# RWKV's beta, k and v turned token-major by 32x32 blocks on VectorE and DMAs, in place of TensorE transposes

## Chip, cores and metric

One NeuronCore of a Trainium2 chip. The metric is the device time of one execution in microseconds; runs are summed up by their median. The engines are PE (TensorE, matrix products), ACT (ScalarE), DVE (VectorE), POOL (GpSimd) and SP (SyncE, which issues nearly all DMAs here).

## What is computed

One layer of a streaming encoder over 512 tokens of width 2048, in float32. An input projection feeds two branches, RWKV-7 time mixing (16 heads of 64) and HGRN2 (8 heads of 128). Their gated outputs go through an output projection, and a layer norm of the residual ends it. Cut to the part that the change touches:

```python
proj = einsum('btd,dc->btc', h, w_in)          # 512 x 2048 by 2048 x 8320
r, k, v, z, wd, ad = split(token_shift(proj[..., :RWKV_COLS]))
kk = normalize(k * k_k);  k = k * (1 + (a - 1) * k_a)
# per head, token by token, state S of 64 x 64:
#   S = S * w_t + (S @ -kk_t) (kk_t * a_t)^T + v_t k_t^T ;  o_t = S @ r_t
y = einsum('btc,cd->btd', concatenate([o_rwkv, o_hgrn], -1), w_out)
out = layer_norm(ALPHA * x + y)
```

The recurrence is evaluated by chunks of 64 tokens. Within a chunk the kernel needs the vectors beta (kk scaled by a and by the decay), k and v with tokens on the partitions, while the projection leaves them with channels on the partitions.

## The kernel before

**Main products.** Projections and the output projection are made in a split form: each operand is a rounded high part and a low rest, and three 128x512 matmuls (line 431, in `three`) make one product. 3900 such matmuls run. Weights come from DRAM in 156 loads of 512 KB (`load`, L408) into two buffers `wr`. Each load is split by halves: ACT makes `wh` (L330), DVE makes `wl` (L340), with three buffers of each. A half feeds 12 main matmuls. A load is issued when the second half of the one two before it is split.

**Side work.** RWKV's heads are treated as 8 pairs, two pairs to a group. `rwkv_prep` makes a pair's operands: `ar` holds kappa and r, `bk` holds beta and k, each [128 channels, 8 chunks, 128]; 16 score products of `bk` and `ar` follow. Then `bk` and v are brought to tokens on partitions (L699 to L729), the latter into rows 64 to 127 of `z`. `rwkv_group` inverts the chunks' triangular matrices by some 60 short DVE operations with block transposes (L359), then `rwkv_scan` walks the 8 chunks, reading `z` and `bk`, and `outputs` and `rwkv_finish` make the gated output `g`. HGRN heads run beside this. For the output projection each gated output is split again into `gh` (tiles named `xh`) and `gl` (`xl`).

**Order.** All instructions are put out by a planner (`Plan`, L63). Python generators yield operations with costs. The planner keeps a clock per engine. Between any two main matmuls it puts out those side operations that would be ready, queue by queue. Engines then run their own lists in order and wait on semaphores. Tiles are taken from counted buffers by `room` and `take`: `q4` has 6 (`ar` and `bk` of two pairs hold 4 until the scan of their group ends, HGRN takes 2), `ksq` 2, `zz` 2, PSUM `mix` and `main` 4 each. The transposes of `bk` and v were PE operations `tr` (L321, against the identity in `cst`) into `mix`, followed by copies (`copy`, L377: ACT or DVE, whichever the planner finds earlier).

**The end.** Pair 7 is prepared last. Its gated output is the last of the 16 that the output projection takes; the first quarter of that projection takes one of them every 12 main matmuls.

Of the kernel before, what the change touches and what calls it, by code (L numbers as in the profile page):

```python
# [15 lines left out]
P = 128  # L16
# [7 lines left out]
NCH = T // C  # L24
# [210 lines left out]
def mixer_kernel(ctx, tc, head, x_r, w_all, par, up, ln_wb, consts, hmask, out):  # L235
    nc = tc.nc
    pe, sc_e, dve, pool = nc.tensor, nc.scalar, nc.vector, nc.gpsimd
# [9 lines left out]
    def nm(s):  # L247
        uid[0] += 1
        return f"{s}{uid[0]}"
# [5 lines left out]
    plan = Plan({**BUFS, **PBUFS})  # L255
    tags = {}

    def st(tag, shape, dt=F32):
        return spool.tile(shape, dt, tag=tag, name=nm(tag), bufs=BUFS[tag])

    def take(tag, shape=(P, T), dt=F32):

        if not plan.free(tag):
            raise RuntimeError(f"no room: {tag}")
        slot = min(plan.slots[tag])
        plan.slots[tag].remove(slot)
        if tag in PBUFS:
            t = ppool.tile(list(shape), dt, tag=tag, name=nm(tag), bufs=PBUFS[tag])
            plan.banks.add(t.tensor.name)
        else:  # L270
            t = st(tag, list(shape), dt)
        name = t.tensor.name
        plan.busy[name] = (slot[1], None)
        tags[name] = tag
        return t

    def drop(*tiles):
        for t in tiles:
            name = t.tensor.name
            plan.slots[tags.pop(name)].append((plan.used.get(name, plan.count), plan.busy[name][0]))  # L280

    def room(**need):

        return lambda: all(plan.free(tag, n) for tag, n in need.items())

    def has(S, *names):
        return lambda: all(n in S for n in names)

    def landed(*tiles):

        names = [getattr(t, "tensor", t).name for t in tiles]

        def test():
            now = plan.clock["pe"] + plan.LEAD
            if not plan.free("mix") or min(plan.slots["mix"])[1] + 0.15 > now:
                return False
            return all(n in plan.ready and plan.seen(n, "pe") <= now for n in names)

        return test


    def size(ap):
        n = 1
        for s in ap.shape[1:]:
            n *= s
        return n
# [13 lines left out]
    def tr(o, i):  # L320
        return Op([("pe", 0.11, lambda: pe.transpose(o, i, ident))], [i], [o])  # L321

    def moved(o, i):

        return 0.1 if o.shape[0] < P else 0.0

    def act_way(o, i, f, scale=1.0, bias=0.0):
        cost = 0.09 + size(o) * 0.00085 + moved(o, i) + (0.06 if isinstance(scale, bass.AP) else 0.0)
        if f == AF.Copy:
            return "act", cost, lambda: sc_e.activation(o, i, f, scale=scale)  # L330
        return "act", cost, lambda: sc_e.activation(o, i, f, scale=scale, bias=bias)  # L331
# [4 lines left out]
    def dve_op(reads, o, f, n=None, per=0.00104, base=0.07):  # L336
        return Op([("dve", base + (n or size(o)) * per, f)], reads, [o])
# [20 lines left out]
    def dtr(o, i):  # L358
        return dve_op([i], o, lambda: dve.transpose(o, i), per=0.0019)  # L359
# [17 lines left out]
    def copy(o, i, scale=1.0):  # L377

        if scale != 1.0:
            f = lambda: dve.tensor_scalar(o, i, scale, None, ALU.mult)  # L380
        else:
            f = lambda: dve.tensor_copy(o, i)
        return Op([act_way(o, i, AF.Copy, scale), ("dve", 0.075 + size(o) * 0.00105 + moved(o, i), f)], [i], [o])

    splits = plan.queue()
# [48 lines left out]
    def by_now(t):  # L436

        n = t.tensor.name
        return n in plan.ready and plan.seen(n, "pe") <= plan.clock["pe"] + plan.LEAD
# [8 lines left out]
    def main_ps(tags=("main",)):  # L448

        def test():  # L450
            now = plan.clock["pe"]
            return [t for t in tags if plan.free(t) and min(plan.slots[t])[1] + 0.15 <= now]

        plan.until(test)
        return take(min(test(), key=lambda t: min(plan.slots[t])[1]))

    def proj(u, hook=None):

        ps = main_ps()
        for j in range(4):  # L460
            if hook:
                hook(j)
            hi, lo = part(4 * u + j, P)
            for kk in range(4):
                if kk == 1:
                    ready(4 * u + j + 1)
                if kk == 2:
                    ready(4 * u + j + 2)
                k = 4 * j + kk
                three(ps, hi[:, kk], lo[:, kk], xh[k], xl[k], k == 0, k == KT - 1)  # L470
        return ps
# [24 lines left out]
    def unit(n=1):  # L496
        u = nunit[0]
        nunit[0] += n
        return u
# [54 lines left out]
    def chunks(t):  # L554
        return t.rearrange("p (c s) -> p c s", s=C)
# [46 lines left out]
    def rwkv_prep(S, p):  # L602
# [5 lines left out]
        bk = take("q4", [P, NCH, 2 * C])  # L608
        a, sg, kx2 = take("t"), take("t"), take("t")
# [6 lines left out]
        for i, (o, xs, low, h) in enumerate(((sg, wah, wlo, HW0), (a, aah, alo, HA0))):  # L616
# [3 lines left out]
            ps = take("mix")  # L620
# [48 lines left out]
        o = S["ot"] = take("t")  # L669
# [17 lines left out]
        pss = [take(tag) for tag in ("main", "mix") for h in range(2)]  # L687
# [8 lines left out]
            drop(ps)  # L696
        S["scored"] = True

        yield room(mix=2)  # L699
        pss = [take("mix") for _ in range(2)]  # L700
        for c in range(NCH):
            yield tr(pss[c // 4][:, c % 4 * P : (c % 4 + 1) * P], bk[:, c])
        for i, ps in enumerate(pss):
            yield copy(bk[:, 4 * i : 4 * i + 4], tiles(ps))
            drop(ps)
        yield has(S, "v")
        yield room(ksq=2)
        rh, rl = (take("ksq", [P, T], F32R) for _ in range(2))
# [6 lines left out]
        v = S["v"]  # L715
# [3 lines left out]

        yield room(zz=1)  # L720
        z = take("zz", [P, NCH, P])
        yield landed(v)
        ps = take("mix")
        for j in range(4):
            yield tr(ps[:, j * P : j * P + P], v[:, j * P : j * P + P])
        for e in range(2):
            yield copy(z[64:128, e::2], tiles(ps)[64 * e : 64 * e + 64])
        drop(ps, v)
        S["zz"] = z  # L729

    def from_v(SS, sc):
# [197 lines left out]
    def tiles(t):  # L929
        return t.rearrange("p (c t) -> p c t", t=P)  # L930
# [239 lines left out]
    pss = [main_ps() for _ in us]  # L1170
# [91 lines left out]
    for name, j in _order()[1:]:  # L1262
# [24 lines left out]
        if name == "k":  # L1287
            plan.add(preps, rwkv_prep(SS[j], j))
            if j % 2 == 1:
                plan.add(groups, rwkv_group(SS[j - 1 : j + 1], j // 2))  # L1290
# [3 lines left out]
        if (name, j) in (("k", 0), ("r", 0)):  # L1294
            ps = pss["wkr".index(name)]
        else:
            ps = proj(unit(), begin_out if (name, j) == ("z", NPAIR - 1) else None)
# [199 lines left out]
    pss = []  # L1497
# [51 lines left out]
    for t in range(4):  # L1549
        sl = slice(t * P, t * P + P)  # L1550
        ps = main_ps(banks if t == 3 else banks)
# [12 lines left out]
        for i in range(2):  # L1564
            c = slice(i * T // 2, i * T // 2 + T // 2)
# [85 lines left out]
```

## Time and profile before

| what | value |
|---|---|
| median of 3 runs | 1061.66 us (1061.06 to 1062.9) |
| profiled execution, its time | 1061.85 us |
| its span | 1060.1 us |
| PE busy | 1052.2 us (99%) |
| DVE busy | 749.0 us (71%) |
| ACT busy | 454.4 us (43%) |
| DMA packets | 35078, of which 4144 under 512 B |

The page gives one profiled execution. Busy times are unions of an engine's instructions; a PE matmul's duration includes its latency, so that matmuls overlap and PE's occupancy is read from the distance of their starts. A row of a group reads: line, engine, operation, tile written <- tiles read, shapes, count, busy us, mean ns, idle time before and what ended it. A row of the timeline begins with the start and the duration in us. A tile is named by its buffer tag, so `t`, `q` (of `q4`) or `ksq` stand for many tensors.

### The profile page before, as it was taken

What the parts mean: (1) busy time and instruction counts of PE and PEld (TensorE: products, weight loads), DVE (VectorE), ACT (ScalarE), POOL (GpSimd) and SP (SyncE); (2) the same over time, 40 slices, a digit from 0 to 9 for tenths busy, and PEclk for the clock granted to TensorE, in tenths of its full rate; (3) what the DMA queues carried; (4) which work ended last, traced back from release to release, by engine and by line L of the source; (5) the groups of instructions that cost most, each with busy time, mean ns of one, the idle gap of its engine ahead of it and who ended that gap; (6) DMA issues with size and microseconds to landing.
All of it is one profiled execution on the core that took longest, in us unless ns stands there. A gap on an engine that the chain in (4) does not pass through costs nothing.

```text
span 1060.1 us, 18788 instructions
## 1 busy us (share of the span) xinstructions
PE 1052.2 (99%) x7438; PEld 875.6 (83%) x7438; DVE 749.0 (71%) x1636; ACT 454.4 (43%) x900; POOL 37.4 (4%) x81
## 2 busy tenths in 40 slices
PE   9999999999999999999999999999999999999997
PEld 8888888888888888888888888888888888888885
DVE  7467995567679977676898556766997878525556
ACT  6455434345353355534533434636335454323321
POOL 0000000000100000001000000000000001000000
PEclk9999999999999999999999999999999999999999
DMA  8222222232233312233232222223332245544613
GB/s 329 56 94 85 84 97 81 71 95 80 76 99 90 100 62 86 70 91 95 90 93 87 82 81 85 80 77 94 89 100 61 81 130 176 172 128 150 208 60 129
DMA packets 35078, 108.46 MB, mean 102 GB/s; under 512 B 4144, under 2 KB 5936, under 8 KB 34864
## 3 DMA queue, kind: packets, MB, share of 16 engines
q1 hardware_dynamic: 34848, 107.08, 32.0%
q8 instruction: 58, 0.95, 0.4%
q14 instruction: 28, 0.23, 0.1%
q10 hardware_dynamic: 144, 0.20, 0.1%
HBM read 99.92 MB, written 7.34 MB: 101 GB/s over the span
## 4 chain that ended last, share of the span: by engine, by line
PE 95%; DMA 2%; DVE 2%; ACT 0%; issue 0%; DVEq 0%
PE main L431 70%; PE mix L317 11%; PE mix L431 8%; PE main L1176 3%; DMA wr<-w_all 2%; PE mix L321 2%; PE main L317 2%; DVE wl L340 0%; PE mix L1126 0%; DVE inv L349 0%; DVE t L340 0%; ACT t L330 0%; DVE inv L340 0%; DVE q L349 0%; DVE ia L340 0%
## 5 line engine op out<-in xcount | busy, mean ns | idle before, releaser
L431 PE MATMUL main<-xh,wl 128*128 128x512 f32 x864 | 342.7, 397 | 0.0
L431 PE MATMUL main<-xh,wh 128*128 128x512 f32 x864 | 342.7, 397 | 0.0
L431 PE MATMUL main<-xl,wh 128*128 128x512 f32 x864 | 340.4, 394 | 0.0
L330 ACT ACTIVATE wh<-wr 128x512 fp32r<-128x512 f32 x299 | 186.9, 627 | 175.1 <-PE main L431 123.9
L340 DVE TENSOR_TENSOR wl<-wr,wh 128x512 fp32r<-128x512 f32 x299 | 204.2, 684 | 76.4 <-ACT wh L330 74.8
L431 PEld LDWEIGHTS main<-xh,wl 128*128 128x128 f32 x864 | 162.5, 188 | 33.0 <-DVE wl L340 0.2
L431 PEld LDWEIGHTS main<-xl,wh 128*128 128x128 f32 x864 | 162.5, 188 | 32.1
L431 PEld LDWEIGHTS main<-xh,wh 128*128 128x128 f32 x864 | 162.6, 188 | 31.0
L431 PE MATMUL main<-wh,xh 128*128 128x512 f32 (+1 forms) x262 | 102.2, 390 | 0.0
L431 PE MATMUL main<-wh,xl 128*128 128x512 f32 (+1 forms) x262 | 102.1, 390 | 0.0
L431 PE MATMUL main<-wl,xh 128*128 128x512 f32 (+1 forms) x262 | 101.8, 389 | 0.1
L431 PEld LDWEIGHTS main<-wl,xh 128*128 128x128 f32 x262 | 49.2, 188 | 10.4 <-DVE wl L340 0.5
L431 PEld LDWEIGHTS main<-wh,xl 128*128 128x128 f32 x262 | 49.2, 188 | 10.0
L431 PEld LDWEIGHTS main<-wh,xh 128*128 128x128 f32 x262 | 49.2, 188 | 9.7
L330 ACT ACTIVATE zz<-mix 64x64 f32<-64x64 f32 (+1 forms) x92 | 25.3, 275 | 57.8 <-PE mix L317 38.8
L331 ACT ACTIVATE t<-main,om 128x512 f32<-128x512 f32 x33 | 22.5, 689 | 44.7 <-PE main L431 35.1
L340 DVE TENSOR_TENSOR inv<-inv 64x30 f32<-64x30 f32 (+14 forms) x120 | 38.7, 322 | 3.2
L340 DVE TENSOR_TENSOR inv<-inv,inv 64x30 f32<-64x30 f32 (+14 forms) x120 | 38.7, 322 | 3.1
L349 DVE SCALAR_TENSOR_TENSOR bd<-mix,pc,bd 64x64 f32<-64x64 f32 x112 | 31.7, 283 | 10.0 <-PE mix L317 8.0
L340 DVE TENSOR_TENSOR t<-t,tot 128x256 f32<-128x256 f32 x96 | 37.1, 419 | 0.3
L349 DVE SCALAR_TENSOR_TENSOR t<-main,pr,t 128x511 f32<-128x511 f32 x33 | 24.4, 746 | 16.9 <-ACT t L331 16.7
L331 ACT ACTIVATE t<-main 128x512 f32<-128x512 f32 x32 | 18.7, 597 | 37.9 <-PE main L431 37.8
(223 smaller groups left out, 1344.8 us busy)
## 6 DMA issues: line engine op xcount, KB each, us to landing
wr<-w_all SPq DMA_DIRECT2D x156, 512.0 KB, 3.6
q<-head SPq DMA_DIRECT2D x15, 448.0 KB, 5.6
g<-x_r SPq DMA_DIRECT2D x16, 256.0 KB, 4.0
spill<-g SPq DMA_DIRECT2D x12, 256.0 KB, 4.5
t<-spill SPq DMA_DIRECT2D x12, 256.0 KB, 4.1
out<-q SPq DMA_DIRECT2D x12, 256.0 KB, 2.5
big<-ln_wb SPq DMA_DIRECT2D x1, 2048.0 KB, 8.7
up<-up SPq DMA_DIRECT2D x8, 128.0 KB, 3.6
```

The source lines that it names most:

```text
L317: return Op([("pe", cost, lambda: pe.matmul(o, l, r, start=start, stop=stop, **kw))], [l, r], [o], mode="narrow" if narrow else "main" if ...
L321: return Op([("pe", 0.11, lambda: pe.transpose(o, i, ident))], [i], [o])
L330: return "act", cost, lambda: sc_e.activation(o, i, f, scale=scale)
L331: return "act", cost, lambda: sc_e.activation(o, i, f, scale=scale, bias=bias)
L340: return dve_op([a, b], o, lambda: dve.tensor_tensor(o, a, b, f), base=0.16 if o.shape[0] < P and size(o) == C and o.tensor.name in tags e ...
L349: return dve_op([a, b], o, lambda: dve.scalar_tensor_tensor(o, a, s, b, f1, f2), per=0.00113, base=0.085 if o.shape[0] == P else 0.25 if s ...
L431: pe.matmul(ps, l, r, start=first and i == 0, stop=last and i == 2)
L1176: pe.matmul(pss[a], *ops, start=k == 0 and low == of == 0, stop=k == KT - 1 and low == 1)
```

## The change

`rwkv_prep` no longer transposes on PE. A new helper, `turned`, transposes every 32x32 block of a tile in one DVE instruction into a scratch tile, and then moves the blocks to their places by DMAs from SP, SBUF to SBUF: 16 DMAs for `bk` (in place, scratch from `q4`) and 8 for v (into rows 64 to 127 of `z`, scratch from `ksq`). Each DMA moves 32 partitions by 8 chunks by 32 floats, 32 KB in rows of 128 B. The planner is told to put out one column of blocks (4 or 2 DMAs), then to let 0.4 us per DMA pass, and takes the result for ready 3.0 us after the last.

```diff
+    def turned(dst, src, tmp, rows=4, base=0):
+        name = dst.tensor.name
+        yield dtr(tmp, src)
+        yield lambda: by_now(tmp)
+        for a in range(4):
+            for b in range(rows):
+                o = base + 32 * b
+                nc.sync.dma_start(dst[o : o + 32, :, 32 * a : 32 * a + 32],
+                                  tmp[32 * a : 32 * a + 32, :, 32 * b : 32 * b + 32])
+            at = plan.clock["pe"] + 0.4 * rows
+            yield lambda: plan.clock["pe"] >= at
+        plan.ready[name] = (plan.clock["pe"] + 3.0, "dma")
...
-        yield room(mix=2)
-        pss = [take("mix") for _ in range(2)]
-        for c in range(NCH):
-            yield tr(pss[c // 4][:, c % 4 * P : (c % 4 + 1) * P], bk[:, c])
-        for i, ps in enumerate(pss):
-            yield copy(bk[:, 4 * i : 4 * i + 4], tiles(ps))
-            drop(ps)
+        yield room(q4=1)
+        tmp = take("q4", [P, NCH, P])
+        yield from turned(bk, bk, tmp)
+        drop(tmp)
...
-        yield landed(v)
-        ps = take("mix")
-        for j in range(4):
-            yield tr(ps[:, j * P : j * P + P], v[:, j * P : j * P + P])
-        for e in range(2):
-            yield copy(z[64:128, e::2], tiles(ps)[64 * e : 64 * e + 64])
-        drop(ps, v)
+        yield room(ksq=1)
+        tmp = take("ksq")
+        yield from turned(z, chunks(v), chunks(tmp), rows=2, base=64)
+        drop(v, tmp)
```

Since the planner decides the order, three places are shown; line numbers after the change are higher by 15 up to the helper's callers.

PE, behind the last score product of pair 0 (`mix_704`), before:

```order
L317 MATMUL mix_704<-q_446,q_447 128x128
L431 MATMUL main_649<-xh_79,wl_661 128x512
L431 MATMUL main_649<-xh_80,wh_680 128x512
L431 MATMUL main_649<-xl_96,wh_680 128x512
L431 MATMUL main_649<-xh_80,wl_681 128x512
L321 MATMUL mix_735<-cst,q_447 128x128 x4
L321 MATMUL mix_736<-cst,q_447 128x128 x4
L431 MATMUL main_649<-xh_81,wh_680 128x512
```

and after:

```order
L317 MATMUL mix_704<-q_446,q_447 128x128
L446 MATMUL main_649<-xh_79,wl_661 128x512
L446 MATMUL main_649<-xh_80,wh_680 128x512
L446 MATMUL main_649<-xl_96,wh_680 128x512
L446 MATMUL main_649<-xh_80,wl_681 128x512
L446 MATMUL main_649<-xh_81,wh_680 128x512
```

The eight transposes of `bk` (`q_447`) are gone and the main matmuls follow one another.

SP's queue around the same pair, with the semaphores that each issue waits for (`DMAHW0` to `DMAHW7` are the eight that DMAs use in turn), before:

```order
L408 DMA wr_685<-w_all 128x1024 [waits DMAHW4_49,DVE_49]
L408 DMA wr_767<-w_all 128x1024 [waits DMAHW5_49,DVE_49]
L408 DMA wr_821<-w_all 128x1024 [waits DMAHW6_49,DVE_49]
L596 DMA up_826<-up 128x256 [waits DMAHW2_49]
L408 DMA wr_876<-w_all 128x1024 [waits DMAHW7_49,DVE_49]
```

and after (the first block DMA waits for PE's scores, which read the tile that it overwrites):

```order
L423 DMA wr_751<-w_all 128x1024 [waits DMAHW5_49,DVE_49]
L394 DMA q_447<-q_735 32x8x32 [waits PE_49]
L394 DMA q_447<-q_735 32x8x32
L394 DMA q_447<-q_735 32x8x32 [waits DMAHW2_49,PE_49]
L394 DMA q_447<-q_735 32x8x32 x3
L394 DMA q_447<-q_735 32x8x32 [waits DMAHW6_49]
L394 DMA q_447<-q_735 32x8x32 [waits DMAHW7_49]
L423 DMA wr_794<-w_all 128x1024 [waits DMAHW0_49,DVE_49]
L394 DMA q_447<-q_735 32x8x32 [waits DMAHW1_49]
L394 DMA q_447<-q_735 32x8x32 [waits DMAHW2_49]
L394 DMA q_447<-q_735 32x8x32 [waits DMAHW3_49]
L394 DMA q_447<-q_735 32x8x32 [waits DMAHW4_49]
```

Eight block DMAs now stand between two weight loads, and each waits for the DMA eight before it.

DVE at the end of the side work, where pair 7's gated output (`g_9174` before) is made and the output projection's splits `wl` and `xl` alternate, before:

```order
L340 TENSOR_TENSOR t_7497<-t_7497,sm_9088 128x512
L340 TENSOR_TENSOR xl_9184<-t_9066,xh_9183 128x512
L349 SCALAR_TENSOR_TENSOR g_9174<-mix_9190,half,t_7405 128x512
L349 SCALAR_TENSOR_TENSOR t_8993<-ksq_9175,t_8993 128x512
L340 TENSOR_TENSOR wl_9202<-wr_9111,wh_9201 128x512
L349 SCALAR_TENSOR_TENSOR g_9174<-g_9174,half,t_8993 128x512
L340 TENSOR_TENSOR xl_9213<-t_9092,xh_9212 128x512
L340 TENSOR_TENSOR wl_9223<-wr_9111,wh_9222 128x512
L340 TENSOR_TENSOR xl_9235<-t_9121,xh_9234 128x512
L340 TENSOR_TENSOR wl_9247<-wr_9171,wh_9246 128x512
```

and after (`g_9369` is the same output):

```order
L340 TENSOR_TENSOR t_7607<-t_7607,sm_9275 128x512
L340 TENSOR_TENSOR wl_9374<-wr_9269,wh_9373 128x512
L349 SCALAR_TENSOR_TENSOR g_9369<-mix_9385,half,t_7437 128x512
L340 TENSOR_TENSOR xl_9393<-g_9241,xh_9392 128x512
L349 SCALAR_TENSOR_TENSOR t_8925<-ksq_9370,t_8925 128x512
L340 TENSOR_TENSOR wl_9406<-wr_9318,wh_9405 128x512
L349 SCALAR_TENSOR_TENSOR g_9369<-g_9369,half,t_8925 128x512
L340 TENSOR_TENSOR xl_9417<-g_9154,xh_9416 128x512
L340 TENSOR_TENSOR wl_9429<-wr_9318,wh_9428 128x512
L340 TENSOR_TENSOR xl_9441<-g_9369,xh_9440 128x512
```

Before, the split `xl` of that output comes further down, behind seven pairs of `xl` and `wl` from the last operation on `g_9174`; after, it is the third row behind it. The finish of the last pair has moved later against the output projection by about six of its steps.

## Prediction

> **What bounds the kernel now.** I read the page first, then the groups of instructions with shapes kept apart, then the transposes' own line, then the timeline around one use of each kind, then SyncE's (SP's) issues.
>
> ```profile
> span 1060.1 us, 18788 instructions
> PE 1052.2 (99%) x7438; PEld 875.6 (83%) x7438; DVE 749.0 (71%) x1636; ACT 454.4 (43%) x900; POOL 37.4 (4%) x81
> DVE  7467995567679977676898556766997878525556
> PE 95%; DMA 2%; DVE 2%; ACT 0%; issue 0%; DVEq 0%
> L431 PEld LDWEIGHTS main<-xh,wl 128*128 128x128 f32 x864 | 162.5, 188 | 33.0 <-DVE wl L340 0.2
> ```
>
> PE is busy for 99% of the span and makes 95% of the chain that ended last. The last row is the check on it: the loads of the low weight halves, which DVE makes, had to wait for DVE 0.2 us in the whole run. The planner keeps PE fed, so what leaves PE leaves the time, unless something else starts to make PE wait. DVE is at 9 tenths in some slices, so there it has little to give.
>
> The profiled execution took 1061.85 us: the span of 1060.1 and 1.75 around it. It lies 0.2 above the median of the runs shown (1061.66); I sum against it. A measurement of this kernel can tell about 0.2%, 2.1 us, from no change.
>
> **What leaves PE.** All transposes stand on one line. The timeline shows one set of eight (beta and k) and one of four (v) on PE, and two splits of weights on ACT that follow PE at its own pace:
>
> ```profile
> L321 PE MATMUL mix<-cst,t x120: 270/272/329, 77.6 to 891.3; 128*128 128x128 f32 x120
> L321 PE MATMUL mix<-cst,q x64: 270/272/273, 72.3 to 751.6; 128*128 128x128 f32 x64
> L321 PEldq EVENT_SEMAPHORE  x13: 51/51/51, 181.1 to 877.7; - x13
> ...
> 105.37 0.39 PE L431 MATMUL main<-xl,wh 128*128 128x512 f32 x1
> 105.59 1.04 PE L321 MATMUL mix<-cst,q 128*128 128x128 f32 x8
> 106.39 0.48 PE L431 MATMUL main<-xh,wl 128*128 128x512 f32 x1
> 106.70 0.40 PE L431 MATMUL main<-xh,wh 128*128 128x512 f32 x1
> ...
> 113.28 0.40 PE L431 MATMUL main<-xh,wl 128*128 128x512 f32 x1
> 113.51 0.60 PE L321 MATMUL mix<-cst,t 128*128 128x128 f32 x4
> 113.87 0.48 PE L431 MATMUL main<-xh,wh 128*128 128x512 f32 x1
> 114.19 0.39 PE L431 MATMUL main<-xl,wh 128*128 128x512 f32 x1
> 907.28 0.63 ACT L330 ACTIVATE wh<-wr 128x512 fp32r<-128x512 f32 x1 [1.56 <-PE main L431]
> 910.00 0.63 ACT L330 ACTIVATE wh<-wr 128x512 fp32r<-128x512 f32 x1 [1.56 <-PE main L431]
> ```
>
> Of the 184 transposes, all 64 of the `q` row and 32 of the `t` row go (8 pairs by 8 and by 4). Their 272 ns is latency, not occupancy: eight take 1.04 us together. What one set costs is read from the starts of the main matmuls. Undisturbed, a half-load of 12 of them lasts 2.72 us (907.28 to 910.00), so they start 0.23 us apart. From 105.37 to 106.70 lie two main starts and eight transposes: 1.33 - 2 x 0.23 = 0.87 us, the slower restart after the switch included. From 113.28 to 114.19: 0.91 - 0.46 = 0.45 us. Eight pairs: 8 x (0.87 + 0.45) = **10.56 us off PE**. The Trainium skill (TensorE: Matmul & The Clock Gate, Part 4: PE-mode transpose) gives about 275 ns for a transpose inside a kernel; taken as PE time, 96 of them would be 26 us and the sum about 1038. The trace agrees with that figure as a duration (272 ns) and not as a price, so the sum goes by the starts.
>
> The copies from PSUM go too. They were off the path.
>
> ```profile
> L330 ACT ACTIVATE q<-mix 128x512 f32<-128x512 f32 x13 | 7.2, 596 | 49.5 <-PE mix L321 49.5
> L330 ACT ACTIVATE zz<-mix 64x512 f32<-64x512 f32 x14 | 8.3, 592 | 18.3 <-PE mix L321 14.2 <-DVE zz L382 4.1
> L359 DVE STREAM_TRANSPOSE inv<-big 32x1024 f32<-32x1024 f32 x8 | 16.3, 2039 | 0.2
> L340 DVE TENSOR_TENSOR wl<-wr,wh 128x512 fp32r<-128x512 f32 x299 | 204.2, 684 | 76.4 <-ACT wh L330 74.8
> ```
>
> ACT loses 15.5 us, worth nothing at 43% busy.
>
> **What DVE gets.** Per pair one block transpose of 1024 columns and one of 512. The nearest row has 1024 columns on 32 partitions, 2.04 us; twice the 512-column row below it would be 1.37. I take 2.04 for 128 partitions, the same operation, and half, 1.02, for v. That is 8 x 3.06 = 24.5 us, less the five copies that ACT did not do, at 0.68 like the other 512-column rows: 3.4. DVE rises by 21 to 770 us, 73%. Its cover is the splitting ahead: three buffers of 2.72 us each are in turn, so a 2.04 us block fits before the next `wl` is due. The HGRN heads take the scratch buffer next, and their first copies, on DVE or ACT in front of the next splits, wait for the last block DMAs: landed 3.6 us after issue at the weights' price (below), freed by the planner after 1.6, so 2 us in each of four groups at most. Where DVE is at 9 tenths it may not. Bounds: nothing, or all that the four odd pairs add (each sits where its group's inversion runs), 4 x 3.06 = 12.2 us. I take 1.0 with this wait in it, near the low end, by the 0.2 us row.
>
> **What SP gets.** 24 DMAs per pair of 32 KB, each waiting for the one eight before it, with weight loads queued behind. The planner spaces them 0.4 us apart.
>
> ```profile
> 13.80 0.53 SPq L529 DMA_DIRECT2D cst<-consts  x1
> 14.38 0.45 SPq L529 DMA_DIRECT2D ksq<-hmask  x1
> ...
> cst<-consts SPq DMA_DIRECT2D x1, 208.0 KB, 5.0
> ksq<-hmask SPq DMA_DIRECT2D x1, 40.0 KB, 4.6
> wr<-w_all SPq DMA_DIRECT2D x156, 512.0 KB, 3.6
> ...
> L408 SPq DMA_DIRECT2D wr<-w_all x156: 327/328/423, 16.9 to 1000.0; - x156
> L1135 SPq DMA_DIRECT2D q<-head x15: 327/328/739, 1.6 to 18.1; - x15
> 351.01 0.33 SPq L408 DMA_DIRECT2D wr<-w_all  x1
> 356.25 0.63 ACT L330 ACTIVATE wh<-wr 128x512 fp32r<-128x512 f32 x1 [2.08 <-PE main L431]
> ```
>
> An issue takes SP 0.33 us, 0.42 when pressed, 0.74 at most. Packets: the mask's 128 rows of 320 B landed at 14.38 + 4.6 = 18.98, the constants queued ahead of them at 18.80; 0.18 us for 8 rows on each of 16 engines, 22 ns a row. A new DMA has 256 rows of 128 B, 16 per engine, at most 0.35 us by that price. So both fit the 0.4 us spacing. How late may a weight load be? The one issued at 351.01 landed at about 354.6, was first read at 356.25 because ACT waited for PE to free a buffer, and its product is due two half-loads later (5.44 us), less the split (0.63 + 0.68): 1.6 + 4.1 = 5.7 us of cover. At 0.42 us an issue, 16 DMAs put SP 0.3 us behind; at 0.74, 5.4 us. I take nothing, with 0 and 20 us as ends (8 pairs by 24 x 0.74 - 9.6 - 5.7 = 2.5).
>
> **What PE gets.** The first products from each `z` now wait for up to eight DMA semaphores. One such wait costs PE's queue 51 ns (row above): 64 of them 3.3 us, or nothing where a 0.23 us matmul runs over them. I take 1.0.
>
> The blocks' own landing is hidden: between the prep of a pair and its scan lies the group's inversion on DVE. In the first group the second pair's v was turned at 113.5, and the scan's first product came at 197.6:
>
> ```profile
> L317 PE MATMUL mix<-rt,big x128: 270/275/347, 197.6 to 867.4; 128*128 128x128 f32 x128
> ```
>
> **The tail.** Pair 7 ends last, and its gated output is the last to be split for the output projection:
>
> ```profile
> 890.96 0.60 PE L321 MATMUL mix<-cst,t 128*128 128x128 f32 x4
> 910.54 0.62 ACT L330 ACTIVATE xh<-g 128x512 fp32r<-128x512 f32 x1
> L349 DVE SCALAR_TENSOR_TENSOR g<-mix,half,t 128x512 f32<-128x512 f32 x16 | 11.9, 747 | 6.7 <-PE mix L321 6.5
> ```
>
> Its last transposes end at 891.56, three DVE operations of 0.75 later (893.8) it is whole, and it is split at 910.54: 16.7 us to spare. In the order of before, seven pairs of `wl` and `xl` stand between; now one (the order shown with the change). Six steps of 2.72 us, 16.3, are gone, since pacing, landing and a fuller DVE push the prep of every pair back. About 0.4 us is left. If the plan is right PE does not wait; I take 0.5, with 0 and 6 (two steps) as ends.
>
> **Sum:** 1061.85 - 10.56 + 1.0 (DVE) + 0 (SP) + 1.0 (semaphores) + 0.5 (tail) = **1053.8 us**. Its own range: 1051.3 with no cost, to 1059 with the tail's 6.
>
> **Rivals.**
> *Weight loads late (slower).* If a block DMA costs SP or the rings c, 16 put SP 16 x (c - 0.4) behind, and beyond 5.7 PE waits, 8 times. The gain is gone at 16 x (c - 0.4) - 5.7 = 1.32, c = 0.84. At c = 1.0 it is 1053.8 + 8 x 3.9 = 1085. For: nothing with 256 rows is in the trace, and small DMAs spread over 32 partitions only. Against: the 0.33 and 22 ns rows. 0.08.
> *Rows of 128 B pay double (slower).* A packet of q1 takes 32.0% x 16 x 1060.1 us / 34848 = 156 ns for 3.07 KB (queue row below), 26 ns for 512 B; if a row of 128 B costs a 512 B read and write, 52 ns, a DMA holds the rings 0.83 us: 16 are 6.9 us behind, 1.2 us of stall a pair, 1063.4 if the queue drains before z, and with z's eight 3.4 us more each, 1091. The Trainium skill (DMA: Bandwidth & Descriptors, Specifications) states 512 B as the least for line rate, with a read-modify-write below. The mask's 320 B rows at 22 ns speak against it here. 0.05.
>
> ```profile
> q1 hardware_dynamic: 34848, 107.08, 32.0%
> ```
>
> *DVE becomes the bound.* All 12.2 us of the odd pairs land on PE: 1061.85 - 10.56 + 12.2 + 1.5 = 1065.0. For: the 9s in DVE's row. Against: 0.2 us of waiting now. 0.10, half of it within 2.1 us since part would still be hidden.
> *The tail decides.* The last group is late by x beyond its 0.4 us and PE waits: 1053.3 + x; x = 8.5 gives 1061.8. For: 16 us of cover spent. Against: the inversion, not a DMA, sets the group's start, and its operations have known times. 0.09, a third each side.
> That the change does nothing is out: the order has 96 transposes fewer.
>
> **Chances.** Forecast 0.68. Faster by over 0.2%: 0.68 + 0.03 = 0.71. Within 0.2%: 0.05 of DVE + 0.03 of the tail = 0.08. Slower: 0.08 + 0.05 + 0.05 + 0.03 = 0.21. The range, 1051 to 1064, holds the forecast, most of the tail and the lower half of the DVE case.
>
> **What would show it.** Right: L321 falls to 88 matmuls, DVE's block transposes rise from 20 to 36, packets to about 87,300 (192 DMAs of 256 rows and 16 semaphores each), PE busy near 1044 and still 99%, and no ACT `wh` group with DMA `wr` among its releasers beyond a few us. Wrong: PE idle before `main` for DVE `wl` (DVE), ACT `wh` waiting for DMA `wr` (SP, rings), an issue of L394 over 0.84 us, or a gap in PE near 890 to 905 ended by `xl<-g` (tail).

## The result and the profile after

Median 1054.11 us (four runs, 1053.71 to 1054.39) against 1061.92 us before (1061.06 to 1062.9): ratio 0.9926, 95% interval 0.9909 to 0.9943, so 7.8 us faster. Measured once more later: 1053.75 against 1061.84, ratio 0.9916 (0.9903 to 0.993). The forecast was 1053.8. The number was right; the experiments show that it was right partly because errors in it cancelled.

The profiled execution of after took 1053.89 us with a span of 1052.1. These are lines of its page, in the order of those shown of before: span, engines, packets, the main queue, and the chain that ended last.

```profile
span 1052.1 us, 18837 instructions
PE 1042.6 (99%) x7342; PEld 867.6 (82%) x7342; DVE 755.1 (72%) x1653; ACT 438.0 (42%) x867; POOL 37.4 (4%) x81
DMA packets 87305, 114.79 MB, mean 109 GB/s; under 512 B 56368, under 2 KB 58160, under 8 KB 87088
q1 hardware_dynamic: 87072, 113.39, 36.5%
PE 99%; DVE 1%; issue 0%; DVEq 0%
```

PE has 96 products fewer and is still busy for 99% of a shorter span: what left PE left the time. DVE rose by 6 us only, where 21 were forecast. The packets are the forecast ones (87,300), and they came cheap: q1's packets took 36.5% x 16 x 1052.1 = 6144 us against 32.0% x 16 x 1060.1 = 5428 before, 717 us more for 52,224 more packets, 14 ns for a row of 128 B. The forecast took 22 as an upper price, and the rival of the double price 52. As an estimate, a quarter of the 26 ns that 512 B of the other packets take would be 6.5, so the short rows cost about twice their share by bytes.

The groups by line and form show the price of each new operation: the block transposes on DVE, and the block DMAs as SP issues them (their line is L394; the weights' DMAs are on L423 now, the main products on L446 and L1185).

```profile
L359 DVE STREAM_TRANSPOSE q<-q 128x1024 f32<-128x1024 f32 x8 | 9.9, 1233 | 0.0
L359 DVE STREAM_TRANSPOSE ksq<-t 128x512 f32<-128x512 f32 x8 | 5.6, 699 | 0.0
```

```profile
L394 SPq DMA_DIRECT2D q<-q x128: 585/608/1749, 75.7 to 769.3; - x128
L394 SPq DMA_DIRECT2D zz<-ksq x64: 585/608/2078, 87.5 to 778.6; - x64
DMA to landing us min/median/max: 1.9/2.5/4.9
```

A block transpose of 1024 columns took 1.23 us, not the 2.04 of the row taken for it. An issue of a block DMA took SP 0.61 us, not 0.33 to 0.42. SP's timeline around the second pair's prep shows what that does to the weights:

```profile
75.67 5.33 SPq L394 DMA_DIRECT2D q<-q  x8
81.10 0.54 SPq L423 DMA_DIRECT2D wr<-w_all  x1
81.69 5.16 SPq L394 DMA_DIRECT2D q<-q  x8
...
87.54 5.96 SPq L394 DMA_DIRECT2D zz<-ksq  x8
```

Eight moves hold SP for 5.2 to 6.0 us where the planner reckoned 3.2, so the weight load behind each eight is late. In the waits, ScalarE's `wh` (the high half of the weights) waits for the weights' DMA six times, 21.5 us together; before it was twice, 3.5 us:

```profile
ACT wh L330 <- DMA wr<-w_all: 21.5, 6, 6.0
PEld mix L317 <- issue: 7.6, 18, 2.1
```

No wait of PE for a weight half follows from it: the lateness ends inside the cover. The second row is the only new stall of PE, 2.1 us in one piece ended by "issue", that is by nothing that the profile shows. It stands in PE's timeline in the middle of a burst of narrow HGRN products (128 products of 16 columns on 32-column weights):

```profile
815.47 0.70 PE L317 MATMUL mix<-t 128*32 128x16 f32 x62
...
816.04 0.45 PE L317 MATMUL mix<-t,t 128*32 128x16 f32 x33
818.54 0.44 PE L317 MATMUL mix<-t,t 128*32 128x16 f32 x29 [2.05 <-issue]
818.90 0.58 PE L446 MATMUL main<-xh,wl 128*128 128x512 f32 x1
...
821.42 0.63 PE L446 MATMUL main<-xh,wh 128*128 128x512 f32 x1
821.85 0.63 PE L446 MATMUL main<-xl,wh 128*128 128x512 f32 x1
...
822.66 0.40 PE L446 MATMUL main<-xh,wh 128*128 128x512 f32 x1
```

After the gap the main products start 0.43 us apart instead of 0.23, half speed, until 822.66. In the trace's packets a transfer of 16 KB on the instruction queue (q8, called a refill below) starts at 816.34, just as PE stops, and ends at 817.27; PE goes on 1.27 us later.

### The profile page after: what moved, and what is told of

It reads as the page before. It is cut to its first block, busy times and chain, and to the rows that moved or that the text cites. A ratio compares the mean times of both kernels' runs of the same rounds, so it can differ in the third digit from the quotient of the medians.

```text
span 1052.1 us, 18837 instructions
## 1 busy us (share of the span) xinstructions
PE 1042.6 (99%) x7342; PEld 867.6 (82%) x7342; DVE 755.1 (72%) x1653; ACT 438.0 (42%) x867; POOL 37.4 (4%) x81
## 3 DMA queue, kind: packets, MB, share of 16 engines
q1 hardware_dynamic: 87072, 113.39, 36.5%
## 4 chain that ended last, share of the span: by engine, by line
PE 99%; DVE 1%; issue 0%; DVEq 0%
PE main L446 74%; PE mix L317 11%; PE mix L446 8%; PE main L1185 3%; PE main L317 2%; PE mix L321 1%; PE mix L1135 0%; DVE inv L349 0%; DVE inv L340 0%; DVE stats L1542 0%; DVEq L1656 0%; DVE mv L1350 0%; DVE mv L345 0%; DVE inv L1133 0%; DVE mv L349 0%
## 5 line engine op out<-in xcount | busy, mean ns | idle before, releaser
L446 PE MATMUL main<-xh,wl 128*128 128x512 f32 x864 | 342.4, 396 | 0.0
L446 PE MATMUL main<-xh,wh 128*128 128x512 f32 x864 | 341.6, 395 | 0.0
L446 PE MATMUL main<-xl,wh 128*128 128x512 f32 x864 | 340.9, 395 | 0.0
L446 PEld LDWEIGHTS main<-xh,wl 128*128 128x128 f32 x864 | 162.7, 188 | 33.0
L446 PEld LDWEIGHTS main<-xl,wh 128*128 128x128 f32 x864 | 162.7, 188 | 32.8
L446 PEld LDWEIGHTS main<-xh,wh 128*128 128x128 f32 x864 | 162.8, 188 | 32.6
L446 PE MATMUL main<-wh,xh 128*128 128x512 f32 (+1 forms) x262 | 102.4, 391 | 0.0
L446 PE MATMUL main<-wh,xl 128*128 128x512 f32 (+1 forms) x262 | 102.1, 390 | 0.0
L446 PE MATMUL main<-wl,xh 128*128 128x512 f32 (+1 forms) x262 | 102.1, 390 | 0.0
L446 PEld LDWEIGHTS main<-wl,xh 128*128 128x128 f32 x262 | 49.2, 188 | 9.8
L446 PEld LDWEIGHTS main<-wh,xl 128*128 128x128 f32 x262 | 49.2, 188 | 9.7
L446 PEld LDWEIGHTS main<-wh,xh 128*128 128x128 f32 x262 | 49.2, 188 | 9.5
L330 ACT ACTIVATE zz<-mix 64x64 f32<-64x64 f32 x61 | 13.4, 219 | 45.6 <-PE mix L317 43.9
```

What stands on the lines that cost most here:

```text
L446: pe.matmul(ps, l, r, start=first and i == 0, stop=last and i == 2)
```

## The experiments

The theory: the gain is PE's own time for the transposes; the moves, DVE and SP are hidden under their covers; the new gap is PE running out of fetched instructions, by the place of the instructions and not by the moves. The rivals: the moves cost PE time through late weights, or make the gap; and DVE is near the bound. Times are medians, beside before on the same chip; ratios have their 95% intervals.

**Another place for the refills** (`pad`).

```diff
-    WARM, T0 = 9, 4.2
+    WARM, T0 = 7, 4.2
...
     for _ in range(WARM):
         pe.matmul(warm, zero, zero)
+    for _ in range(32):
+        pe.matmul(warm[:32, :16], zero[:, :32], zero[:, :16])
```

> Theory: the one new stall of the changed kernel, 2.05 us at 816.5 to 818.5 in the middle of a burst of 128 narrow HGRN products, is TensorE's instruction queue being refilled (a transfer of that queue starts at 816.34), and the half-speed matmuls after it (818.9 to 822.3, some 1.8 us lost) follow from it. Where a refill falls depends only on how many instructions stand ahead. Two warming matmuls fewer and 32 narrow products more at the start move every later instruction by 30 matmuls and the order of the rest stays. Then the stall is gone from 816 and the time falls by 3.8 us, less some 0.35 for the products: about 1050.3 us, unless the shifted refill now falls inside another of the bursts, which would show as the same gap elsewhere and about 1054. Rival: the stall comes from the block DMAs or from the ring; then it stays where it is, and the time stays 1054.1 to 1054.5.

Measured: 1051.65 us against 1062.52, ratio 0.9903 (0.989 to 0.9917). The timeline of its profile at the same burst, and its waits:

```profile
817.22 0.70 PE L317 MATMUL mix<-t,t 128*32 128x16 f32 x62
817.85 0.50 PE L446 MATMUL main<-xh,wl 128*128 128x512 f32 x1
...
820.06 0.39 PE L446 MATMUL main<-xh,wh 128*128 128x512 f32 x1
```

```profile
PEld mix L317 <- issue: 6.2, 19, 0.4
```

The gap is gone with every block DMA still there, and so is the half speed. The same stretch, from the first main product behind the burst to the eighth, lasts 2.21 us here (817.85 to 820.06) and 3.76 in after (818.90 to 822.66): the half speed cost 1.55 us beside the gap's 2.05. The time came down less than expected because the padding costs more than the 0.35 us I gave it; that needed a control.

**The padding alone, in the kernel before** (`pad_before`, the same edit).

> The same padding in the kernel before, which has no refill stall in a burst. Theory: the padding by itself costs, and what it won in the changed kernel was the stall. It puts the first real product 1.6 us later (6.53 instead of 4.91 us after the start, in the padded changed kernel) and saves at most 0.5 us of slow first products: 1.1 to 1.6 us slower than before, about 1063.3. Rival: the padding wins by itself, by a better warmed clock or a luckier start: 2 to 3 us faster than before, about 1059.5, as it did in the changed kernel.

Measured: 1064.01 us (eight executions, 1063.48 to 1068.03) against 1061.95, ratio 1.0028 (1.0017 to 1.0039), 2.1 us slower. So the padding wins nothing by itself. In the changed kernel it made up for its 2.1 us and 2.4 more (1054.1 to 1051.65): 4.5 us, the gap, the half speed and a start at full speed.

**The changed kernel again,** unchanged (`after_again`).

> The changed kernel unchanged, for more executions and a second profile. Theory: the gap near 816 comes with the place of the instructions, so it is there again, 2 to 2.5 us in the second half of the same burst of narrow products, and the time is 1053.7 to 1054.5 in most executions; where half speed does not follow the gap, 1051.9 to 1052.7. Rival: the gap is chance; then the second profile has none, and the executions spread from 1050 to 1054.

Measured: 1053.75 us against 1061.84, ratio 0.9916 (0.9903 to 0.993). The second profile has the gap at the same product, here too behind the thirty-third of the row:

```profile
815.71 0.45 PE L317 MATMUL mix<-t,t 128*32 128x16 f32 x33
818.49 0.62 PE L317 MATMUL mix<-t,t 128*32 128x16 f32 x29 [2.33 <-issue]
```

Its five executions lie in two groups, 1053.75 to 1053.88 and 1052.02 and 1052.31, 1.6 us apart, about what the half speed costs, and their granted clocks lie in the same groups: 0.998 and 1.000. The gap goes with the place; by the clocks, whether half speed follows differs between executions (of these five, only one of the first group was profiled).

That the gap is a refill is inferred, since no view shows the instructions that PE holds, but the traces of all runs agree on it. They have nine gaps of over 0.2 us of PE that end by "issue" (one each in after, `after_again`, `no_moves`, `pace` and `v_look1`, two each in `dve2` and `split_moves`). In each of them PE goes on 1.22 to 1.51 us after the end of a 16 KB transfer of q8, of which there are only 58 in 1052 us.

**The moves left out** (`no_moves`). Beta and k's block DMAs go and v's are replaced by two of 64 partitions; the block transposes and the order on PE, DVE and ACT are those of after.

```diff
-                nc.sync.dma_start(dst[o : o + 32, :, 32 * a : 32 * a + 32],
-                                  tmp[32 * a : 32 * a + 32, :, 32 * b : 32 * b + 32])
+                if rows == 2 and a in (0, 2) and b == 0:
+                    h = a // 2
+                    nc.sync.dma_start(dst[64:128, :, 64 * h : 64 * h + 64], tmp[64 * h : 64 * h + 64])
```

> The block transposes on VectorE stay, the block DMAs of beta and k are left out, and v is moved by two DMAs of 64 partitions, so the blocks lie in the wrong places and the result is not the reference's. Theory: the moves are hidden, SyncE is 3.3 us behind after 16 issues of 0.61 us and the weights have 5.7 us of cover: the time stays within 0.5 us of the changed kernel's 1054.1, and only ScalarE's wait for the weights' DMA goes down from 21.5 us towards the 3.5 us of before; 3.8 us less if the one instruction refill in a burst happens to fall elsewhere, which the profile shows. Rival: the moves still cost TensorE time through late half-loads (the smallest lead of a low weight half over its product was 0.26 us): then 3 to 6 us faster with the gap near 816 still there.

Measured: 1053.49 us against 1062.52, ratio 0.9916 (0.9902 to 0.9929). Its executions too lie in two groups (1051.91 and 1052.7; 1054.27 and 1054.56). Its waits and its timeline, in the execution of 1052.7:

```profile
PEld mix L317 <- issue: 8.6, 20, 2.4
ACT wh L330 <- DMA wr<-w_all: 3.3, 2, 1.7
```

```profile
815.14 0.57 PE L317 MATMUL mix<-t,t 128*32 128x16 f32 x47
818.03 0.31 PE L317 MATMUL mix<-t,t 128*32 128x16 f32 x15 [2.32 <-issue]
818.28 0.50 PE L447 MATMUL main<-xh,wl 128*128 128x512 f32 x1
818.61 0.40 PE L447 MATMUL main<-xh,wh 128*128 128x512 f32 x1
```

ScalarE's wait is back at 3.3 us and the time is the same: 18 us of waiting on ScalarE were worth nothing. And the gap stands in a kernel without the moves, 14 products further on. The moves neither cost PE anything that shows here nor make the gap. Here full speed follows it (0.33 us from 818.28 to 818.61, where after has 0.39 and then 0.43).

**Twice the issues** (`split_moves`). Each block DMA cut in two: the same rows and bytes.

```diff
+                for h in range(2):
+                    c = slice(4 * h, 4 * h + 4)
+                    nc.sync.dma_start(dst[o : o + 32, c, 32 * a : 32 * a + 32],
+                                      tmp[32 * a : 32 * a + 32, c, 32 * b : 32 * b + 32])
```

> Every block DMA is cut in two of half the rows: 384 DMAs of 128 rows of 128 B where there were 192 of 256, the same bytes and rows. Theory A, an issue costs by its rows: 128 rows cost SyncE the 0.33 us of a weight load's 128 rows, 32 issues 10.5 us against 9.7 before, 4.1 us behind the pacing of 6.4, still inside the cover of 5.7: 1054 to 1056 us. Theory B, an issue of this kind costs a fixed 0.61 us: 32 take 19.5 us, 13.1 behind, 7.4 beyond the cover, 8 times: 59 us, about 1113, with ScalarE waiting for the weights' DMA and TensorE behind it. Halfway (0.47 us each): 15.0 us, 8.6 behind, 2.9 beyond, 23 us: about 1077.

Measured: 1140.84 us against 1062.52, ratio 1.0746 (1.0731 to 1.0761). An issue of 128 rows costs what one of 256 did (first row below, issues of L396; the second is sixteen of them in SP's timeline):

```profile
L396 SPq DMA_DIRECT2D q<-q x256: 585/599/1492, 75.6 to 862.7; - x128
```

```profile
75.58 10.39 SPq L396 DMA_DIRECT2D q<-q  x16
```

The waits show where that goes: PE for `wh` as expected, and about as much for `ksq` from DVE. Three views follow: the waits, PE's timeline at the longest of these (the product before it starts at 99.54), and DVE's at the same time.

```profile
ACT wh L330 <- DMA wr<-w_all: 125.4, 22, 13.3
PE main L448 <- ACT wh L330: 28.5, 9, 5.8
PE mix L317 <- DVE ksq L340: 26.2, 7, 10.5
```

```profile
110.41 0.79 PE L317 MATMUL mix<-ksq,ones_r 128*128 128x512 f32 x1 [10.46 <-DVE ksq L340]
111.00 0.63 PE L448 MATMUL main<-xh,wl 128*128 128x512 f32 x1
111.43 0.63 PE L448 MATMUL main<-xh,wh 128*128 128x512 f32 x1
```

```profile
109.66 0.69 DVE L340 TENSOR_TENSOR ksq<-pf,ksq 128x512 fp32r<-128x512 f32 x1 [6.87 <-DMA zz<-ksq]
110.27 0.68 DVE L340 TENSOR_TENSOR wl<-wr,wh 128x512 fp32r<-128x512 f32 x1
```

That is theory B with a second path. DVE stands 6.87 us in front of `ksq`, whose buffer the block DMAs of z still read, and the next `wl` stands behind it. It is the scratch-buffer wait that the prediction had put into DVE's term at 2 us a group: real, and in after 0.3 us, once. The measured cost is above the 59 us of theory B. PE's waits for `wh`, `ksq` and, with 2.2 and 2.1 us, for `wl` and `uph` add up to 59.0, but 26.2 of them came by `ksq`, a path that theory B did not have: that its figure is met is partly luck. The stall shown is followed by products at half speed (111.00 to 111.43), and the mean granted clock is 0.974 against 0.998: 0.024 x 1138.6 = 27 us. As an estimate, 59 + 27 = 86, and the spans (1138.6 and 1052.1) are 86.5 apart.

**One half alone.** Beta and k by blocks with v on PE (`bk_only`), and the reverse (`v_only`, twice more as `v_look1` and `v_look2`, and with the padding as `v_pad`); in each the other half's code is that of before.

> Beta and k by blocks as in the changed kernel, v by TensorE transposes as before. Theory: the gain is TensorE's own time, 0.87 us a pair for the eight transposes of beta and k and 0.45 for the four of v: 8 x 0.87 = 7.0 us of gain, about 1054.9 us against 1061.9 of before, 3.8 us less if no instruction refill falls in a burst, and up to 1.5 us less for the switches between products that go with the transposes. Rival: v's moves or waits ate v's share of the gain, so that leaving v alone costs nothing: 1054.1 or below with a refill inside a burst still in the profile.

Measured: 1055.53 us against 1062.52, ratio 0.9936 (0.9923 to 0.9948): 7.0 us of gain, as reckoned. No gap of a refill shows in its profile; the longest wait ended by "issue" is 0.4 us. But the profile has a new wait and a slow start:

```profile
PE mix L317 <- DVE ksq L340: 0.9, 1, 0.9
```

```profile
7.88 0.85 PE L1188 MATMUL main<-xh,t 128*128 128x512 f32 x3
```

The product of the second view starts at 7.29 in before. So a span that is 6.4 us shorter (1053.7 against 1060.1) holds 0.9 of waiting and 0.6 of half speed that before does not have: 7.9 us came off PE, and that the median shows the 7.0 reckoned is partly luck.

> The other half: v by blocks, beta and k by TensorE transposes. Theory: gains add, 8 x 0.45 = 3.6 us, about 1058.3, where beta and k alone gave 7.0; a refill stall in a burst would show in the profile and cost 2 to 4. Rival: part of v's gain is lost to waits of z's products for the block DMAs, 64 waits of 51 ns: 0.4 us of gain, about 1061.5.

Measured: 1061.09 us against 1061.95, ratio 0.999 (0.9982 to 0.9999): 0.9 us of gain, not 3.6. A miss. The profiled execution took 1059.54 us, 2.4 below before, and shows the rest in two new waits and a slow start (the last row; 7.29 in before):

```profile
449.88 0.49 PE L317 MATMUL mix<-zz,q 128*128 128x128 f32 x2 [0.72 <-ACT zz L330]
...
885.94 0.63 PE L321 MATMUL mix<-cst,t 128*128 128x128 f32 x4 [0.30 <-DVE t L340]
```

```profile
8.08 0.86 PE L1188 MATMUL main<-xh,t 128*128 128x512 f32 x3
```

The span is 2.5 us shorter (1057.6 against 1060.1); with 1.0 for the waits and 0.8 for the start, 4.3 us came off PE in this execution, and none of v's 3.6 is missing.

> v alone once more, unchanged, for a second look: its first profiled execution took 1059.5 us and the others up to 1062.0. Theory: an execution near 1061 shows the missing time as a refill gap inside a burst of narrow products or as half-speed matmuls behind it or at the start (1 to 2.5 us), with the rest as in the first profile. Rival: it shows TensorE waiting for z's block DMAs or for weights, spread over the pairs.

> The same kernel and the same expectation, for a third execution.

Measured: one execution each, 1060.58 and 1059.56 us. Both have the two waits, 1.0 us together. The slower one also has a gap of 0.54 us inside a burst of narrow products, up to 833.34, which the other two profiled executions of the same program do not have; none has PE (its matmuls) waiting for the block DMAs or for weights. The same sum as above gives 3.9 and 3.8 us off PE.

> v alone by blocks, with the same padding at the start. v alone won 0.9 us where 3.6 were forecast. Theory: the missing 2.7 us are instruction refills and half-speed matmuls that fall differently in each execution, not v's moves: with another alignment the refills fall elsewhere and the time lies at 1061.9 - 3.6 + 2.1 (what the padding cost in the kernel before) = 1060.4 or below, that is below v alone. Rival: v's moves or their waits really eat 2.7 us: then it is slower than v alone by the padding's 2.1, about 1063.2.

Measured: 1060.87 us, before 1061.82, ratio 0.9999 (0.999 to 1.0008), in which its slower executions weigh. Six of eleven lie at 1060.3 to 1060.9, the others at 1062.8 to 1064.2; the profiled one (1063.82) is of the upper group and has eleven main products at half speed at its start. The rival wanted 1063.2 as the middle and gets it only where half speed is seen; the theory's 1060.4 lies in the lower group. Inconclusive for the median. In the profiles nothing is missing: 3.8 to 4.3 us came off PE in the three of v alone, and 1.0 (two new waits, neither for the moves) and 0.2 to 0.8 (the start) went back. Why most executions of v alone are up to 2.5 us slower than the one of 1059.54 was caught only in part, in `v_look1`.

**Twice DVE's share** (`dve2`).

```diff
         yield dtr(tmp, src)
+        yield dtr(tmp, src)
```

> Every block transpose on VectorE is done twice, into the same buffer: 16 more, 8 x (1.23 + 0.70) = 15.5 us more of VectorE, 771 us in all, which is what the prediction took for the changed kernel. Theory: VectorE's work is covered by the splitting ahead, so the time stays within 1 us of 1054.1 (up to 4 us below if the refill stall falls away). Rival: VectorE is close to the bound in the stages where the odd pairs' prep meets an inversion: 4 x 1.93 = 7.7 us slower, about 1062, with TensorE waiting for wl from VectorE.

Measured: 1052.42 us against 1061.95, ratio 0.9916 (0.9903 to 0.9929). DVE is busy for 766.5 us, 11 more than in after, since the planner gave ScalarE some copies:

```profile
PE 1042.5 (99%) x7342; PEld 866.7 (82%) x7342; DVE 766.5 (73%) x1658; ACT 441.5 (42%) x878; POOL 37.6 (4%) x81
```

The rival's 7.7 us do not come: DVE is not the bound. (The order on PE shifts too, and the gap near 816 with it.) That nothing at all is lost is not shown: with that gap gone the time is still 1.2 us above `pace` below. The profile, of the slowest of the four executions (1055.27), has one wait of PE for DVE that after does not have, 1.24 us for `bd` up to 846.37. The doubled work does not explain it: the last block transpose starts at 786.4, and DVE itself had just waited 2.26 us for ACT.

**The price told to the planner** (`pace`).

```diff
-            at = plan.clock["pe"] + 0.4 * rows
+            at = plan.clock["pe"] + 0.61 * rows
```

> The planner is told the measured price of an issue: 0.61 us for each block DMA instead of 0.4, so the weight loads are no longer planned behind a SyncE that is 3.3 us late. Theory: the late loads cost nothing in the changed kernel, so ScalarE's wait for the weights' DMA falls from 21.5 us to below 10 and the time stays within 1 us of 1054.1 (up to 4 below if the refill stall falls away, which the profile shows). Rival: the late loads cost something through smaller leads of wl (21 of 250 half-loads under 1.5 us): 1 to 3 us faster with a refill stall still there.

Measured: 1051.27 us against 1061.95, ratio 0.99 (0.9887 to 0.9912), the fastest of all with `pad`. Its waits and the one gap in its timeline, at three large products just behind a burst:

```profile
ACT wh L330 <- DMA wr<-w_all: 11.0, 6, 2.7
```

```profile
834.85 0.60 PE L317 MATMUL mix<-zz,q 128*128 128x128 f32 x3
836.42 0.27 PE L317 MATMUL mix<-zz,q 128*128 128x128 f32 x1 [0.98 <-issue]
```

ScalarE's wait is halved (to 11.0, a little over the 10 expected). The span is 3.1 us shorter than after's: 1.1 by the smaller gap (0.98 for 2.05), 1.55 by the half speed that does not follow it, and the start, where the product that after starts at 7.95 comes at 6.92, has more than the remaining 0.45. Nothing is left over that an earlier weight load would have to explain, and `no_moves`, where no load is late, is no faster.

## Why the prediction was right, point by point

**What leaves PE: right as the cause, 10.56 us a little small.** Taking out the transposes of beta and k alone gave what the starts of the main products said (7.0 us at the median of `bk_only`, 7.9 off PE in its profile). For the whole: the span fell by 8.0 us, and after also carries 2.05 us of gap, 1.55 of half speed behind it and 0.65 of half speed at its start. The start is read from the first products in both timelines:

```profile
4.91 2.50 PE L1185 MATMUL main<-xh,t 128*128 128x512 f32 x6
...
7.95 0.86 PE L1185 MATMUL main<-xh,t 128*128 128x512 f32 x3
```

```profile
4.91 1.85 PE L1176 MATMUL main<-xh,t 128*128 128x512 f32 x6
...
7.29 0.91 PE L1176 MATMUL main<-xh,t 128*128 128x512 f32 x3
```

(after first, before second: 7.95 against 7.29 for the same product.) 8.0 + 2.05 + 1.55 + 0.65 = 12.2 us came off PE, 1.7 more than forecast. The halves account for it: 7.9 (`bk_only`) and 4.3 (`v_only`) are 12.2, so that each was forecast too small, by 0.9 and 0.7. The samples were not at fault: taken from the starts in the trace of before in the same way, each of the eight sets of eight costs 0.88 us, and each set of four that stands alone between two main products 0.44 to 0.46. What else goes with a set was not isolated. The price of 272 ns a transpose (26 us in all) was rightly refused.

**DVE: 1.0 us forecast, nothing found.** The rate was wrong: 1.23 and 0.70 us an operation, 15.5 us in all and not 24.5. The row that I took has 32 partitions and other strides; twice the 512-column row, which I had beside it (1.37), was nearer. DVE rose by 6.1 us in all: five copies of `q` and `zz` out of PSUM left it, as reckoned, and the planner, which the forecast did not follow that far, also exchanged smaller copies between DVE and ACT. `dve2` shows that even twice the work costs none of the rival's 7.7 us and at most about 1, so the cover was the right argument and the bound of 12.2 far too wide.

**SP: nothing forecast, nothing found, by another sum.** The issue costs 0.61 us, above the 0.33 to 0.42 taken for it and inside the end of 0.74. Sixteen take 9.7 us against 6.4 planned: 3.3 late, of a cover of 5.7. The cover is what held. `split_moves` used it up, and the rival's own formula with the measured price then gave 59 us of lateness before the slow clock. The statement that ScalarE would not wait beyond a few us was wrong (21.5), and harmless (`no_moves`; `pad`, with 28.5 us of it, is among the fastest).

**PE's semaphores: 1.0 us forecast, nothing found.** `no_moves` has the waits for two moves a pair instead of 24. The span of its profiled execution (1050.9) is 1.2 us shorter, less than the 2.4 of half speed that after's has and it has not (1.55, and 0.86 at the start: 7.95 against 7.09).

**The tail: 0.5 us forecast, nothing found.** No row of PE near 890 to 905 in after waits for `xl`. The step of the prediction that left 0.4 us of cover was not tested further.

**What was not forecast:** the gap, and the half speed behind it: 3.6 us, with the start 4.25. The three costs that did not come (2.5) and the 1.7 more off PE stand against it, 4.2. That is why 1053.8 was met to 0.3 us: the direction and the main term were reasoned, the closeness is luck. With the refills in other places the same change gives 1051.3 (`pace`).

**The rivals.** Weights late: the mechanism is real at twice the issues (`split_moves`; nothing between was run), not here. Double price for 128 B rows: refuted by 14 ns a row. The Trainium skill (DMA: Bandwidth & Descriptors, Why small descriptors are slow (HBM only)) says that transfers between places in SBUF escape the penalty of small rows; the 14 ns, under the 26 that 512 B take, agree with it as far as they go, and so speak against reading the section that I had cited for the rival (Specifications) on these moves. DVE and the tail: not met.

## What to carry to other kernels

On a kernel whose bound engine is never idle, the price of an operation there is the shift of its neighbours' starts, and its removal is worth about that (12.2 us here for the 10.6 so read). Small moves were paid in issues here, not in bytes (`split_moves`): count them times the issue's measured time, hold that against how late a load on the same queue may be, and tell the planner the real figure (by itself this was worth nothing that shows here: `pace`'s gain is that of the gap, the half speed and the start). A change of a few us also moves where instruction refills fall, which here was worth 2 to 4 us either way; before a small gain or loss is put down to the edit, look for gaps ended by "issue" in bursts of short products, and pad once to see them move.

## What the runs showed of the hardware

- An SP issue of a move between places in SBUF took 0.60 to 0.61 us whether it had 256 rows (after), 128 (`split_moves`) or 512 (`no_moves`, 602/612/710 ns), against 0.33 for a weight load over 128 partitions.
- A block transpose of 128 x 1024 fp32 took 1.23 us where both sides are whole rows, and 2.01 on 32 partitions with the inversion's strides.
- PE ran dry for 2.05 to 2.33 us in a burst of short products, at the same product in two executions of one program, within 0.15 us of the start of a 16 KB transfer of the instruction queue. All nine gaps of PE of over 0.2 us that end by "issue" end 1.22 to 1.51 us after such a transfer does. Not every refill that starts in a burst does this: in before one starts at 395.61 inside one and nothing waits. What decides it stayed open.
- A gap of 2.05 and 2.33 us was followed by half speed for 3 to 4 us in both profiles of after, and one of 2.32 us by none in `no_moves`; the two groups of times in both kernels fit that it differs between executions. The Trainium skill (TensorE: Matmul & The Clock Gate, Part 1) ties half speed to about 3.4 us of idleness, in a window that runs free of the kernel; here shorter gaps, among narrow products, were enough. From the last main product ahead of the burst to the first behind it are 3.8 us in after (815.14 to 818.90), 4.2 in `after_again` and 4.0 in `no_moves`, so the page's figure would fit if the narrow products counted for little; no run tests that. That the slow start differs between executions, as the page says, shows here too: the same product starts at 7.95 and 7.59 in the two profiles of after, and over all kernels 0 to 11 main products are slow.
